# A convolutional feed-forward stage on one NeuronCore: both halves' sample products in one visit, with joins and splits put elsewhere

## The chip, the core and the metric

The kernel runs on one NeuronCore of a Trainium2 chip. A core has five engines that run their own instruction streams: TensorE (PE in the profile; PEld is its weight load), VectorE (DVE), ScalarE (ACT), GpSimd (POOL) and SyncE (SP, which here only issues DMAs). They wait for each other by semaphores. The metric is the device time of one execution in microseconds (us). The kernel before takes 1741.15 us, the median of three runs (1740.54 to 1743.8).

## The reference

One step of a one-layer hybrid decoder: 256 prompt tokens and 64 sample tokens (8 sequences of 8), model width 2048. The first part mixes tokens (a chunked gated MLP beside a state-space scan); the change does not touch its arithmetic. The second part is the convolutional feed-forward, with 5632 hidden columns:

```python
def conv_ffn(h, conv_state, w_up, conv_w, conv_b, w_down):
    up = h @ w_up
    up, new_conv = causal_depthwise_conv(up, conv_state, conv_w, conv_b)
    g, u = jnp.split(up, 2, axis=-1)
    return (jax.nn.gelu(g, approximate=True) * u) @ w_down, new_conv
...
    f, new_ffn_conv = conv_ffn(rms_norm(x, p["norm_ffn_pre"]), ffn_conv_state,
                               p["ffn_w_up"], p["ffn_conv_w"], p["ffn_conv_b"], p["ffn_w_down"])
    x = x + rms_norm(f, p["norm_ffn_post"])
```

Everything is float32. The convolution has three taps; its last two rows of each sequence are outputs too.

## The kernel before

**Products in parts.** A float32 matmul is done as three matmuls of rounded parts. ScalarE rounds a weight slab to its high part (`whi`, line 124), VectorE subtracts to get the low part (`wlo`, line 125), and TensorE adds up high by high, low by high and high by low (lines 135 to 137). `slab` loads a slab on SP's queue; `rounded` and `split_after` put the splits in an order on their engine, with no semaphore.

**Groups.** The feed-forward goes in 11 groups (`NG`) of 4 x 128 hidden columns. `ffn_up(g)` makes the up projection of both halves (gate and value) of group g: 16 parts of 24 matmuls (`ps`). Each finished block of 128 columns goes through `evac`: VectorE scales it out of PSUM into `pad` (lines 1346, 1347), ScalarE and VectorE do the convolution (1353, 1355), GpSimd copies the kept rows (`stg` 1357, `ptf` 1358), and in the value half VectorE multiplies gate and value into the left operand `a` (1363, prompt) and `a_s` (1364, samples). A store of `stg` (1405) stands on ScalarE's queue. `Parts` cuts `a` into four blocks a11, a12, a21, a22 and four sums s1 to s4, each split into a high part on ScalarE (398) and a low part on VectorE (399).

**The down projection** of group g-1 runs between the parts of group g: after each part, `advance` takes one step of the generator `down_steps(g - 1, ...)`. The output has 2048 columns in two halves m. For each half, prompt tokens take seven products instead of eight (a Strassen-like scheme): p1 (a11 by b11), p2 (a12 by b21), p5 (s1 by t1), p7 (s3 by t3), p3 (s4 by b22), p6 (s2 by t2), p4 (a22 by t4). b11 to b22 are blocks of the down weights (128 x 1024 each, on SP's queue); t1 to t4 are differences of them, each made by four subtractions on GpSimd (`less`, line 1512), which are ordered behind the last copy of kept rows (`kept_rows`). One product is `ready` (split of the weights, 1490 and 1491), six matmuls into `pm` (1475), and an add on VectorE into one of seven running sums (`taken_in`, 1469). The sample tokens take no such scheme: at p2's step of each half the raw weights are multiplied by `a_s` in eight matmuls (`pms`, 1482, two records each in the profile). In this text that is a **visit**. Two visits a group, ten groups, make 20.

t3 overwrites b12, t2 overwrites b11 and t4 overwrites b21; b11, b12, b21 and b22 are read by the visit too, so GpSimd makes t2, t3 and t4 only after it.

**The end.** After the last group, `together` joins the seven running sums of each half (seven adds of 128 x 512 on VectorE, line 1567): half 0 after its last product, half 1 at the end of the last `down_steps`. The last group has no later group to hide behind: `down_plain` does its down products straight (lines 1572 and on), with slabs split by line 124 and 125, and the final RMSNorm follows (1700, 1720).

**What sets the order.** Each engine's order is fixed when the program is built, by priorities: `first()` and `tc.high_priority` raise one, `tc.issue_after(x)` puts an instruction behind x on its engine. The lines that the prediction turns on:

```python
for i, (xi, wi) in enumerate(((0, 0), (1, 0), (0, 1))):   # whi by a_hi, whi by a_lo, wlo by a_hi
...
elif j == 3:
    self.cut("a12")
    self.cut("a22")
```

## Time and profile before

The profiled execution took 1738.82 us; its span is 1737.1 us.

| | |
|---|---|
| median, lowest, highest of three runs | 1741.15, 1740.54, 1743.8 us |
| profiled execution, span | 1738.82, 1737.1 us |
| TensorE, VectorE, ScalarE, GpSimd busy | 1722.9, 1363.9, 878.5, 684.8 us |
| sample matmuls `pms`, 320 records | 73.1 us |
| weight subtractions on GpSimd, line 1512, 320 | 351.1 us in three groups |
| DMA traffic | 310.6 MB, 179 GB/s mean |

Rows of a timeline are: start, duration, engine, line, operation, tiles written <- tiles read, shape, count, and in brackets the idle time just before and what ended it. Rows of the chain of waits are: start, time on the chain, engine, tile, line. Rows of the windows are: stretch, its length, then busy time and instructions of PE, PEld, DVE, ACT and POOL, TensorE's granted clock, the DMA share and GB/s. Of two overlapping matmuls each has its own full duration, so the distance of their starts is what one costs.

### The profile page before, as it was taken

What the parts mean: (1) busy time and instruction counts of PE and PEld (TensorE: products, weight loads), DVE (VectorE), ACT (ScalarE), POOL (GpSimd) and SP (SyncE); (2) the same over time, 40 slices, a digit from 0 to 9 for tenths busy, and PEclk for the clock granted to TensorE, in tenths of its full rate; (3) what the DMA queues carried; (4) which work ended last, traced back from release to release, by engine and by line L of the source; (5) the groups of instructions that cost most, each with busy time, mean ns of one, the idle gap of its engine ahead of it and who ended that gap; (6) DMA issues with size and microseconds to landing.
All of it is one profiled execution on the core that took longest, in us unless ns stands there. A gap on an engine that the chain in (4) does not pass through costs nothing.

```text
span 1737.1 us, 29944 instructions
## 1 busy us (share of the span) xinstructions
PE 1722.9 (99%) x11223; PEld 1605.9 (92%) x11223; DVE 1363.9 (79%) x2137; ACT 878.5 (51%) x1272; POOL 684.8 (39%) x999
## 2 busy tenths in 40 slices
PE   9999999999999999999999999999999999999997
PEld 9999999999999999999988898888888889888884
DVE  6549864657969788788987778888887879798898
ACT  6344545333656565645565444444444444454443
POOL 2432230000423423112355556565655555555552
PEclk9999999999999999999999999999999999999999
DMA  8786664556676777665765544545445454545445
GB/s 265 215 240 184 185 177 148 157 163 191 202 225 197 227 221 220 205 199 164 241 185 156 158 147 148 159 142 178 150 145 171 144 166 150 164 149 160 148 143 161
DMA packets 216018, 310.60 MB, mean 179 GB/s; under 512 B 22080, under 2 KB 118976, under 8 KB 215680
## 3 DMA queue, kind: packets, MB, share of 16 engines
q1 hardware_dynamic: 198624, 279.76, 53.1%
q0 software_dynamic: 6176, 13.87, 2.6%
q10 hardware_dynamic: 11072, 15.05, 2.5%
q8 instruction: 88, 1.44, 0.4%
q14 instruction: 58, 0.48, 0.1%
HBM read 285.00 MB, written 22.32 MB: 177 GB/s over the span
## 4 chain that ended last, share of the span: by engine, by line
PE 96%; DVE 2%; issue 1%; ACT 0%; POOL 0%; DVEq 0%; ACTq 0%; POOLq 0%
PE ps L135 20%; PE ps L137 20%; PE ps L136 20%; PE pm L1475 11%; PE pd L135 4%; PE pd L137 4%; PE pd L136 4%; PE pms L1482 4%; PE y_ps L1088 1%; PE ps_v L135 1%; PE ps_v L136 1%; PE ps_v L137 1%; DVE wlo L125 0%; PE yo_ps L1003 0%; PE up_ps L1020 0%
## 5 line engine op out<-in xcount | busy, mean ns | idle before, releaser
L135 PE MATMUL ps<-h_hi,whi 128*128 128x320 f32 x2428 | 750.2, 309 | 0.0
L137 PE MATMUL ps<-h_hi,wlo 128*128 128x320 f32 x2428 | 749.0, 309 | 0.1
L136 PE MATMUL ps<-h_lo,whi 128*128 128x320 f32 x2428 | 748.6, 308 | 0.0
L125 DVE TENSOR_TENSOR wlo<-wraw,whi 128x1024 fp32r<-128x1024 f32 (+2 forms) x394 | 487.4, 1238 | 146.0 <-ACT whi L124 144.2
L124 ACT CAST whi<-wraw 128x1024 fp32r<-128x1024 f32 (+2 forms) x393 | 405.1, 1031 | 372.9 <-PE ps L136 143.1
L135 PEld LDWEIGHTS ps<-h_hi,whi 128*128 128x128 f32 x2428 | 455.6, 188 | 9.1 <-issue 1.3
L136 PEld LDWEIGHTS ps<-h_lo,whi 128*128 128x128 f32 x2428 | 455.9, 188 | 6.3
L137 PEld LDWEIGHTS ps<-h_hi,wlo 128*128 128x128 f32 x2428 | 455.5, 188 | 0.7 <-DVE wlo L125 0.6
L1491 DVE TENSOR_TENSOR wlo<-b,whi 128x1024 fp32r<-128x1024 f32 x120 | 155.1, 1292 | 74.4 <-ACT whi L1490 74.2
L1490 ACT CAST whi<-b 128x1024 fp32r<-128x1024 f32 x120 | 125.5, 1046 | 161.9 <-PE ps L136 144.1
L1512 POOL TENSOR_TENSOR b<-b,b 128x256 f32<-128x256 f32 x160 | 184.8, 1179 | 0.0
L135 PE MATMUL pd<-ohi,whi 128*128 128x320 f32 x448 | 138.7, 310 | 0.0
L137 PE MATMUL pd<-ohi,wlo 128*128 128x320 f32 x448 | 138.3, 309 | 0.0
L136 PE MATMUL pd<-olo,whi 128*128 128x320 f32 x448 | 138.3, 309 | 0.0
L1358 POOL COPY ptf<-pad 128x2 f32<-128x2 f32 x88 | 39.2, 446 | 187.2 <-DVE pad L1346 186.6
L1512 POOL TENSOR_TENSOR b<-b,t 128x256 f32<-128x256 f32 x80 | 76.8, 969 | 86.0 <-PE pms L1482 86.0
L1512 POOL TENSOR_TENSOR t<-b,b 128x256 f32<-128x256 f32 x80 | 89.5, 1148 | 14.7 <-DMA b<-in_ffn_w_down 14.7
L135 PEld LDWEIGHTS pd<-ohi,whi 128*128 128x128 f32 x448 | 84.1, 188 | 0.6
L136 PEld LDWEIGHTS pd<-olo,whi 128*128 128x128 f32 x448 | 84.1, 188 | 0.3
L137 PEld LDWEIGHTS pd<-ohi,wlo 128*128 128x128 f32 x448 | 84.1, 188 | 0.0
L248 DVE TENSOR_TENSOR acc_mix<-acc_mix,pd 128x320 f32<-128x320 f32 (+1 forms) x113 | 53.7, 478 | 27.8 <-PE pd L137 27.5
L1482 PE MATMUL pms<-b,a_s 128*64 128x512 f32 x320 | 73.1, 598 | 0.0
(415 smaller groups left out, 2490.4 us busy)
## 6 DMA issues: line engine op xcount, KB each, us to landing
wraw<-in_ffn_w_up SPq DMA_DIRECT2D x176, 512.0 KB, 4.5
wraw<-in_w_in SPq DMA_DIRECT2D x132, 512.0 KB, 3.9
b<-in_ffn_w_down SPq DMA_DIRECT2D x80, 512.0 KB, 4.5
wraw<-in_w_out SPq DMA_DIRECT2D x64, 512.0 KB, 3.5
st<-in_state_ssm SPq DMA_DIRECT2D x40, 256.0 KB, 4.4
out_ssm_state_sample<-st ACTq DMA_DIRECT2D x30, 256.0 KB, 2.4
cs<-dacs_d SPq DMA_DIRECT2D x16, 320.0 KB, 5.3
wraw<-in_w_in SPq DMA_DIRECT2D x12, 384.0 KB, 4.3
```

The source lines that it names most:

```text
L124: rounded[:] = [act.copy(hi, raw).ins]
L125: lowered[:] = [dve.tensor_tensor(out=lo, in0=raw, in1=hi.bitcast(F32), op=ALU.subtract).ins]
L135: pe.matmul(ps, whi, xhi, start=first, stop=False)
L136: pe.matmul(ps, whi, xlo, start=False, stop=False)
L137: last_made[0] = pe.matmul(ps, wlo, xhi, start=False, stop=last).ins
L248: added_last[:] = [dve.tensor_tensor(out=acc[:, nb, ts], in0=acc[:, nb, ts], in1=ps[:, ts], op=ALU.add).ins]
L1358: kept_rows[:] = [pool.tensor_copy(ptf[:, k, :], pad[:, 256:258]).ins]
L1475: last_made[0] = pe.matmul(ps, x[xi][:, k], w[wi][:, 512 * k:512 * k + 512], start=start and k + i == 0, stop=stop and k == 1 and i == 2).ins
L1482: last_made[0] = pe.matmul(ps[64 * h:64 * h + 64], a_s[:, k0 + k], w[h][:, 512 * k:512 * k + 512], start=start and k == 0, stop=stop and k ...
L1490: rounded[:] = [act.copy(hi, raw).ins]
L1491: dve.tensor_tensor(out=lo, in0=raw, in1=hi.bitcast(F32), op=ALU.subtract)
L1512: pool.tensor_tensor(out=to[:, cs], in0=raw[x][:, cs], in1=raw[y][:, cs], op=ALU.subtract)
```

## The change

1. **One visit a group.** Both halves' sample products are done at the second half's p2 step, 16 matmuls. So the first half's four weight blocks stay unwritten until then: t1 to t4 go to tiles of their own (`one`, `two`), and the second half's b11 lies in an extension of the first running sums' tile (`beside`), b12 and b22 in the two `gain` tiles, b21 in t1's tile. Their loads are issued at the end of the first half's steps.
2. **Weight differences behind the last copy of kept rows.** The `ptf` copy now comes ahead of the `stg` copy, and `less` is ordered behind the latter.
3. **Joins one or two to a step.** The joins of the last `down_steps` are put into its steps, each with `first()`; the last group's evacuations of blocks 2 and 3 of the value half are ordered behind the latest one.
4. **Last chunk.** Slab splits from the fourth on are ordered behind the last left operand's split; the last group's two stores of kept rows wait for its first split on ScalarE; the loads of the norm's gain move into the last `down_steps`; raw tiles are used in another order.
5. Four scratch tiles of the earlier part (`sq`, `s`, `zs`) come from another pool, which frees room in SBUF.

The diff, without the moves of item 5:

```diff
@@ -1332,7 +1333,11 @@
             parts = Parts(a, a_s, g == NG - 1)
 
             def evac(half, j, ps):
-                with first() if g == NG - 1 and half == 1 else nullcontext():
+                with ExitStack() as how:
+                    if g == NG - 1 and half == 1:
+                        how.enter_context(first())
+                        if j >= 2:
+                            how.enter_context(tc.issue_after(taken[0]))
                     convolved(half, j, ps)
 
             def convolved(half, j, ps):
@@ -1354,8 +1359,8 @@
                 for r in range(1, 3):
                     dve.scalar_tensor_tensor(out=t[:, :n], in0=pad[:, r:r + n], scalar=col(prm_at[f"fw{r}"][0] + k), in1=t[:, :n],
                                              op0=ALU.mult, op1=ALU.add)
-                pool.tensor_copy(stg[:, half, j], tokp[:, :, 8:10])
-                kept_rows[:] = [pool.tensor_copy(ptf[:, k, :], pad[:, 256:258]).ins]
+                with tc.issue_after(pool.tensor_copy(ptf[:, k, :], pad[:, 256:258]).ins):
+                    kept_rows[:] = [pool.tensor_copy(stg[:, half, j], tokp[:, :, 8:10]).ins]
                 if half == 0:
                     gelu[:] = [act.activation(t[:, :n], t[:, :n], AF.Gelu_apprx_tanh).ins]
                     return
...
@@ -1402,7 +1407,8 @@
 
             for half in range(2):
                 k = NF * half + 4 * g
-                act.dma_start(o_fconv_s[:, k:k + 4], stg[:, half])
+                with tc.issue_after(parts.made[0]) if g == NG - 1 else nullcontext():
+                    act.dma_start(o_fconv_s[:, k:k + 4], stg[:, half])
             return parts
 
         eps = fp.tile([P, 1], F32, name="eps")
@@ -1453,11 +1460,13 @@
 
         nxt = ffn_up(0)
 
-        sums_of_m, f_s, taken = [None, None], [None, None], []
+        sums_of_m, f_s, taken, beside, gain = [None, None], [None, None], [], [], []
 
         def room_for_sums(m):
 
-            room = fp.tile([P, 8, 512], F32, name="in_fp") if m else hp.tile([P, 8, 512], F32, tag="acc_mix", name="in_mix")
+            room = fp.tile([P, 8, 512], F32, name="in_fp") if m else hp.tile([P, 10, 512], F32, tag="acc_mix", name="in_mix")
+            if m == 0:
+                beside.append(room[:, 8:10].rearrange("p i n -> p (i n)"))
             sums_of_m[m] = [room[:, i] for i in range(7)]
             f_s[m] = room[:, 7]
 
@@ -1492,88 +1501,119 @@
...
+            def samples():
+                ps = [misc("pms") for _ in range(2)]
+                for h in range(2):
+                    raw = raws[h]
+                    sample_products(ps[h], parts.a_s, 0, (raw["b11"], raw["b12"]), True, False)
+                    sample_products(ps[h], parts.a_s, 2, (raw["b21"], raw["b22"]), False, True)
+                for h in range(2):
+                    taken_in(f_s[halves[h]], ps[h], ck == 0)
+
...
-                for name in ("b11", "b12", "b22", "b21"):
-                    load(name)
-                product(1, "a11", "b11")
+            for name in ("b11", "b12", "b22", "b21"):
+                load(0, name, fp.tile([P, 1024], F32, name=name))
+            for h in range(2):
+                raw = raws[h]
+                last = h and ck == NG - 2
+                if last:
+                    together(0, 0)
+                product(h, 1, "a11", "b11")
                 yield
-                raw["t1"] = fp.tile([P, 1024], F32, name="t1")
-                less(raw["t1"], "b12", "b11")
-                ps = misc("pms")
-                sample_products(ps, parts.a_s, 0, (raw["b11"], raw["b12"]), True, False)
-                sample_products(ps, parts.a_s, 2, (raw["b21"], raw["b22"]), False, True)
-                taken_in(f_s[m], ps, ck == 0)
-                product(2, "a12", "b21")
+                one = fp.tile([P, 1024], F32, tag="t2" if h else "t1", name="one")
+                less(h, "t1", "b12", "b11", one)
+                if h:
+                    samples()
+                if last:
+                    together(0, 1)
+                product(h, 2, "a12", "b21")
                 yield
-                raw["t3"] = raw["b12"]
-                less(raw["t3"], "b22", "b12")
-                product(5, "s1", "t1")
+                two = beside[0] if h else fp.tile([P, 1024], F32, tag="t2", name="two")
+                less(h, "t3", "b22", "b12", two)
+                if last:
+                    together(0, 2)
+                product(h, 5, "s1", "t1")
                 yield
-                raw["t2"] = raw["b11"]
-                less(raw["t2"], "b22", "t1")
-                product(7, "s3", "t3")
-                if ck == 0 and m == 1:
+                less(h, "t2", "b22", "t1", one)
+                if last:
+                    together(0, 3)
+                product(h, 7, "s3", "t3")
+                if ck == 0 and h == 0:
                     with tc.issue_after(lowered[0]):
                         to_rows(2)
                 yield
-                raw["t4"] = raw["b21"]
-                less(raw["t4"], "t2", "b21")
-                product(3, "s4", "b22")
-                if ck == 0 and m == 1:
+                less(h, "t4", "t2", "b21", two)
+                if last:
+                    together(0, 4, 5)
+                product(h, 3, "s4", "b22")
+                if ck == 0 and h == 0:
                     with tc.issue_after(lowered[0]):
                         to_rows(3)
+                if last:
+                    with tc.issue_after(slab_load[-1]):
+                        for m in range(2):
+                            gain.append(fp.tile([P, SN, 4, 32], F32, tag="gain", name="gain", bufs=2).rearrange("p s k f -> p (s k f)"))
+                            sp.dma_start(gain[m][:, :1024], norm_last[0:1, 1024 * m:1024 * m + 1024].broadcast_to([P, 1024]))
                 yield
-                product(6, "s2", "t2")
+                if last:
+                    together(0, 6)
+                    together(1, 1)
+                product(h, 6, "s2", "t2")
+                if h == 0:
+                    if ck == 0:
+                        room_for_sums(halves[1])
+                    load(1, "b11", beside[0])
+                    for name in ("b12", "b22"):
+                        load(1, name, fp.tile([P, SN, 4, 32], F32, tag="gain", name=name, bufs=2).rearrange("p s k f -> p (s k f)")[:, :1024])
                 yield
-                product(4, "a22", "t4")
-                if ck == NG - 2 and m == 0:
-                    together(0)
+                if last:
+                    together(1, 0, 2, 3, 4)
+                product(h, 4, "a22", "t4")
+                if h == 0:
+                    load(1, "b21", fp.tile([P, 1024], F32, tag="t1", name="b21"))
+                if last:
+                    together(1, 5, 6)
                 yield
-            if ck == NG - 2:
-                together(1)
-                yield
 
...
-        def together(m):
+        def together(m, *which):
             t = [None] + sums_of_m[m]
...
+            sums = ((6, 1, ALU.add), (2, 1, ALU.add), (7, 6, ALU.add), (6, 5, ALU.add), (3, 6, ALU.add), (4, 7, ALU.subtract), (7, 5, ALU.add))
+            for n in which:
+                x, y, op = sums[n]
+                with first(), tc.issue_after(taken[0]):
+                    taken[:] = [dve.tensor_tensor(out=t[x], in0=t[y], in1=t[x], op=op).ins]
+            if 6 in which:
+                for c, n, i in ((0, 0, 2), (0, 1, 3), (1, 0, 4), (1, 1, 7)):
+                    f[c][2 * m + n] = t[i]
@@ -1597,7 +1637,8 @@
                             kept = [fp.tile([P, 1024], F32R, tag=t, name="kept") for t in ("b11", "b12")]
                         elif (nb, i) in ((1, 1), (3, 1)):
                             kept = [held_w[:, nb - 1], held_w[:, nb]]
-                        raw = None if 3 <= n < 6 else fp.tile([P, 1024], F32, tag=("t1", "b22", "b21")[n % 6], name="raw")
+                        raw = None if 3 <= n < 6 else fp.tile([P, 1024], F32, tag=("b22", "b21", "t1")[n % 6], name="raw")
+                        split_after.append(parts.made if n >= 3 else None)
                         slab(rows_of(ffn_w_down, 4 * ck + 2 * i, 2, 512 * nb, 512), kept=kept, room=raw)
                         w = tuple(kept or both[1:])
                         raws.append(both[0])
@@ -1658,11 +1698,6 @@
             nxt = ffn_up(g)
             while bg:
                 advance(bg, steps)
-            if g == 4:
-                with tc.issue_after(slab_load[-1]):
-                    for m in range(2):
-                        gain.append(fp.tile([P, SN, 4, 32], F32, tag="gain", name="gain", bufs=2).rearrange("p s k f -> p (s k f)"))
-                        sp.dma_start(gain[m][:, :1024], norm_last[0:1, 1024 * m:1024 * m + 1024].broadcast_to([P, 1024]))
 
         held_w = hp.tile([P, 4, 1024], F32R, tag="h_hi", name="held_w")
         gain_s = hp.tile([P, 1024], F32, tag="ohi", name="gain_s")
@@ -1756,7 +1791,8 @@
         with tc.issue_after(gelu[0]):
             act.activation(fp.tile([P, 1], F32, name="root_ready"), eps, AF.Sqrt)
         down_plain(NG - 1, nxt, one_block, load_x1)
-        act.dma_start(o_fconv_p, ptf)
+        with tc.issue_after(nxt.made[0]):
+            act.dma_start(o_fconv_p, ptf)
 
 
 _OUTS = [
```

The orders of three engines at the start of the group whose weights are b_12648 (b11), b_12650 (b12), b_12652 (b22) and b_12654 (b21). In the trace this is the group with its first product at 1203.19 us, and the other six from 1036.55 to 1536.47 us stand alike.

TensorE, before, between two parts at p2's step of the first half:

```order
L137 MATMUL ps_3_12557<-h_hi,wlo 128x320
L1482 MATMUL pms<-b_12648,a_s 64x512
L1482 MATMUL pms<-b_12650,a_s 64x512
L1482 MATMUL pms<-b_12648,a_s 64x512
L1482 MATMUL pms<-b_12650,a_s 64x512
L1482 MATMUL pms<-b_12654,a_s 64x512
L1482 MATMUL pms<-b_12652,a_s 64x512
L1482 MATMUL pms<-b_12654,a_s 64x512
L1482 MATMUL pms<-b_12652,a_s 64x512
L1475 MATMUL pm<-whi,a_hi 128x512
L1475 MATMUL pm<-whi,a_lo 128x512
```

In the changed kernel p2 stands directly behind the part:

```order
L137 MATMUL ps_3_12557<-h_hi,wlo 128x320
L1484 MATMUL pm<-whi,a_hi 128x512
L1484 MATMUL pm<-whi,a_lo 128x512
L1484 MATMUL pm<-wlo,a_hi 128x512
L1484 MATMUL pm<-whi,a_hi 128x512
```

The eight matmuls between are now in the second half's visit, ahead of eight of its own.

GpSimd, before, from the last copies of kept rows on (`t_12698` is t1; `b_12650<-b_12652,b_12650` is t3):

```order
L1358 COPY ptf<-pad 128x2
L1512 TENSOR_TENSOR t_12698<-b_12650,b_12648 128x256 x4
L1357 COPY stg<-pad 128x16
L1343 MEMSET pad 128x2
L1344 COPY pad<-fst 128x8x2
L1343 MEMSET pad 128x2
L1344 COPY pad<-fst 128x8x2
L1343 MEMSET pad 128x2
L1344 COPY pad<-fst 128x8x2
L1512 TENSOR_TENSOR b_12648<-b_12652,t_12698 128x256
L1512 TENSOR_TENSOR b_12650<-b_12652,b_12650 128x256 x2
```

And in the changed kernel (first `one` is t1, first `two` is t3):

```order
L1362 COPY ptf<-pad 128x2
L1363 COPY stg<-pad 128x16
L1519 TENSOR_TENSOR one<-b_12650,b_12648 128x256 x4
L1519 TENSOR_TENSOR two<-b_12652,b_12650 128x256 x4
L1348 MEMSET pad 128x2
L1349 COPY pad<-fst 128x8x2
L1348 MEMSET pad 128x2
L1349 COPY pad<-fst 128x8x2
L1348 MEMSET pad 128x2
L1349 COPY pad<-fst 128x8x2
L1519 TENSOR_TENSOR one<-b_12652,one 128x256 x4
```

The stg copy moved ahead of t1, and t3's four subtractions moved up behind t1's.

VectorE, in the changed kernel, up to the split of a12 (the first of `a_lo ... x2`):

```order
L1443 TENSOR_TENSOR s<-a 128x256
L1443 TENSOR_TENSOR s<-s,a 128x256
L1500 TENSOR_TENSOR wlo<-b_12654,whi 128x1024
L1478 TENSOR_TENSOR in_mix<-in_mix,pm 128x512
L125 TENSOR_TENSOR wlo<-wraw,whi 128x1024
L399 TENSOR_TENSOR a_lo<-a,a_hi 128x256 x2
L1443 TENSOR_TENSOR s<-a,s 128x256
L399 TENSOR_TENSOR s_lo<-s,s_hi 128x256 x2
L1500 TENSOR_TENSOR wlo<-one,whi 128x1024
L1478 TENSOR_TENSOR in_mix<-in_mix,pm 128x512
```

These rows stand as before (with other line numbers); only the add of `pms`, which followed behind them, is gone from here.

More of the change, by code (lines that the diff above doesn't have):

```diff
@@ L105, in first @@
         return tc.high_priority(offset=200000)
-    slab_load, split_after, both, rounded, lowered = [], [None], [], [], []
+    slab_load, split_after, both, rounded, lowered, copied = [], [None], [], [], [], []
     def slab(src, half=0, begins=False, kept=None, room=None):
@@ L328, in add_square @@
         else:
-            sq = tp.tile([P, NT], F32, tag=place[0], name="sq", bufs=place[1])
+            sq = mixer[0].tile([P, NT], F32, tag=place[0], name="sq", bufs=place[1])
             act.activation(sq, x, AF.Square)
@@ L347, in step @@
                 else:
-                    one.append(tp.tile([P, NT], F32, tag="sq", name="sq", bufs=2))
+                    one.append(mixer[0].tile([P, NT], F32, tag="sq", name="sq", bufs=2))
                 for ts in parts_of(nb):
@@ L397, in split @@
         if scale is None:
-            act.copy(hi, x)
+            copied[:] = [act.copy(hi, x).ins]
             made = dve.tensor_tensor(out=lo, in0=x, in1=hi.bitcast(F32), op=ALU.subtract)
@@ L1494, in down_steps, with load @@
             last_rows = kept_rows[0]
+            halves = (1, 0) if ck == 0 else (0, 1)
+            raws = [{}, {}]
+            def load(h, name, room):
+                k, n = int(name[1]) - 1, int(name[2]) - 1
+                raws[h][name] = room
+                with tc.high_priority(offset=100000), tc.issue_after(slab_load[-1]) if ck == 0 else nullcontext():
+                    sp.dma_start(room.rearrange("p (k n) -> p k n", n=512),
+                                 rows_of(ffn_w_down, 4 * ck + 2 * k, 2, 1024 * halves[h] + 512 * n, 512))
@@ new lines, in less, with product @@
+            def less(h, to, x, y, room):
+                raw = raws[h]
+                with tc.high_priority(offset=100000), tc.issue_after(last_rows):
+                    for q in range(0, 1024, 256):
+                        cs = slice(q, q + 256)
+                        pool.tensor_tensor(out=room[:, cs], in0=raw[x][:, cs], in1=raw[y][:, cs], op=ALU.subtract)
+                raw[to] = room
+            def product(h, i, x, w):
+                hi, lo = ready(raws[h][w])
+                ps = misc("pm")
+                prompt_products(ps, (parts.hi[x], parts.lo[x]), (hi, lo), True, True)
+                taken_in(sums_of_m[halves[h]][i - 1], ps, ck == 0)
@@ L1558, in down_steps @@
+                yield
+                if last:
[5 more added lines that the diff above has]
+                    together(1, 5, 6)
                 yield
         f = [[None] * 4 for _ in range(2)]
-        def together(m):
+        def together(m, *which):
             t = [None] + sums_of_m[m]
-            def plus(x, y, op=ALU.add):
-                with tc.issue_after(taken[0]):
-                    dve.tensor_tensor(out=t[x], in0=t[y], in1=t[x], op=op)
-            plus(6, 1)
-            plus(2, 1)
-            plus(7, 6)
-            plus(6, 5)
-            plus(3, 6)
-            plus(4, 7, ALU.subtract)
-            plus(7, 5)
-            for c, n, i in ((0, 0, 2), (0, 1, 3), (1, 0, 4), (1, 1, 7)):
-                f[c][2 * m + n] = t[i]
+            sums = ((6, 1, ALU.add), (2, 1, ALU.add), (7, 6, ALU.add), (6, 5, ALU.add), (3, 6, ALU.add), (4, 7, ALU.subtract), (7, 5, ALU.add))
[6 more added lines that the diff above has]
+                    f[c][2 * m + n] = t[i]
```

33 lines of the change are left out of this document (9 added, 24 removed).

## The prediction

> **What bounds the kernel now.** I read the page first, then the windows by stage, the chain of waits, and the timelines of TensorE, VectorE and GpSimd at the places the change touches.
>
> ```profile
> PE 1722.9 (99%) x11223; PEld 1605.9 (92%) x11223; DVE 1363.9 (79%) x2137; ACT 878.5 (51%) x1272; POOL 684.8 (39%) x999
> PE 96%; DVE 2%; issue 1%; ACT 0%; POOL 0%; DVEq 0%; ACTq 0%; POOLq 0%
> 873.00:1600.00 727.00, 727.00 (x4352) 645.32 (x4352) 602.92 (x841) 357.42 (x447) 412.50 (x568) 1.00 0.51 157
> ```
>
> TensorE (PE) is the bound, and in the stage that the change edits (873 to 1600 us, the feed-forward groups) it is busy for all 727.00 us. So a matmul less there is time gained one to one, and a wait put before a matmul there is time lost one to one, with nothing behind it to win it back. VectorE is second, 602.92 of 727.00 us, so it has little room wherever its work comes in a lump.
>
> **The visits.** Per half, the sample products are 16 records in one piece between two parts of other work. The chain at the start of the group whose first product is at 1203.19:
>
> ```profile
> 1203.19 1.39 PE pm L1475 x6
> 1208.09 3.58 PE pms L1482 x16
> 1211.67 1.60 PE pm L1475 x6
> 1216.79 1.39 PE pm L1475 x6
> ```
>
> A visit costs 3.58, and the product after it 1.60 instead of 1.39, so 3.79 us. Inside, two records go together:
>
> ```profile
> 1208.50 0.60 PE L1482 MATMUL pms<-b,a_s 128*64 128x512 f32 x2
> 1208.93 0.60 PE L1482 MATMUL pms<-b,a_s 128*64 128x512 f32 x2
> 1209.36 1.89 PE L1482 MATMUL pms<-b,a_s 128*64 128x512 f32 x8
> ```
>
> 0.43 us per pair, eight pairs 3.44, so entering and leaving cost 3.79 - 3.44 = 0.35 us. The change does 32 records in one visit: 0.35 us less in each of nine groups. In the order of the new program the first group's visit is still in two pieces (13 matmuls, then 3 after other work), so it saves nothing. **Visits: 9 x 0.35 = -3.15 us.** That is all TensorE saves; its matmuls are the same in number.
>
> **What the first visit was covering.** The second product of a half (a12 by b21, "p2") came behind the visit. Now it comes directly behind the part before it. The step from product to product without a visit is 1216.79 - 1211.67 - 0.21 = 4.91 us, so p2 starts at 1203.19 + 4.91 = 1208.10, where before it came at 1211.67. Its second matmul multiplies whi by the low half of a12, 0.23 us later: it needs a_lo at 1208.33. VectorE (DVE) makes that a_lo here:
>
> ```profile
> 1207.95 1.22 DVE L125 TENSOR_TENSOR wlo<-wraw,whi 128x1024 fp32r<-128x1024 f32 x1
> 1209.09 0.42 DVE L399 TENSOR_TENSOR a_lo<-a,a_hi 128x256 fp32r<-128x256 f32 x1
> 1036.55 1.39 PE pm L1475 x6
> 1042.44 1.28 DVE L399 TENSOR_TENSOR a_lo<-a,a_hi 128x256 fp32r<-128x256 f32 x2
> 1536.47 1.39 PE pm L1475 x6
> 1542.37 1.29 DVE L399 TENSOR_TENSOR a_lo<-a,a_hi 128x256 fp32r<-128x256 f32 x2
> ```
>
> It ends at 1209.51: 1.18 us after p2 now wants it, where the visit used to hide that (ready 2.4 us before the old need). The third and fourth rows and the last two show the same distance, 5.9 us from first product to a_lo, in the first and the last of the seven groups from 1036.55 to 1536.47 in steps of 83.3 us. VectorE's order there is unchanged by the change: the low weights of p2, an add, the low weights of a slab, then a_lo. What is late next is the slab part behind p2, whose low weights come before a_lo and so add nothing.
>
> Can VectorE be there earlier? Only by losing a wait ahead of it:
>
> ```profile
> 1199.00:1209.50 10.50, 10.50 (x67) 9.19 (x67) 10.40 (x22) 7.29 (x12) 3.03 (x5) 1.00 0.24 75
> 1198.56 0.57 DVE L1355 SCALAR_TENSOR_TENSOR ucv<-pad,prm,ucv 128x336 f32<-128x336 f32 x1 [0.57 <-ACT ucv L1353]
> 1197.86 0.67 ACT L1353 ACTIVATE ucv<-pad,prm 128x336 f32<-128x336 f32 x1 [4.37 <-POOL stg L1357]
> ```
>
> It is busy 10.40 of 10.50 us to that point. One wait, 0.57, is for ScalarE (ACT), which stood behind a store that waited for GpSimd's stg copy. The change puts that copy ahead of the weight subtractions, so the 0.57 and the 0.1 of small gaps go: -0.67.
>
> But the change also frees the third weight difference of the half (t3) from waiting for the visit, and gives it a tile of its own. Its four GpSimd (POOL) subtractions now run straight behind t1's four, where before they came at 1209:
>
> ```profile
> 1192.17 4.84 POOL L1512 TENSOR_TENSOR t<-b,b 128x256 f32<-128x256 f32 x4
> 1209.18 0.92 POOL L1512 TENSOR_TENSOR b<-b,t 128x256 f32<-128x256 f32 x1 [3.75 <-PE pms L1482]
> 1190.13 1.22 DVE L125 TENSOR_TENSOR wlo<-wraw,whi 128x1024 fp32r<-128x1024 f32 x1
> 1192.25 1.74 DVE L125 TENSOR_TENSOR wlo<-wraw,whi 128x1024 fp32r<-128x1024 f32 x1
> 1193.91 0.67 DVE L1469 TENSOR_TENSOR in_fp<-in_fp,pm 128x512 f32<-128x512 f32 x1
> 1194.51 1.21 DVE L125 TENSOR_TENSOR wlo<-wraw,whi 128x1024 fp32r<-128x1024 f32 x1
> 1195.65 0.75 DVE L1364 TENSOR_TENSOR a_s<-ucv,gcv 128x64 f32<-128x64 f32 x1
> 1200.64 0.22 DVE L1364 TENSOR_TENSOR a_s<-ucv,gcv 128x64 f32<-128x64 f32 x1
> ```
>
> While GpSimd subtracts, a VectorE operation on two SBUF tiles loses about 0.53: wlo takes 1.74 instead of 1.22, a_s 0.75 instead of 0.22; the add out of PSUM stays at 0.67. Four more subtractions between 1197 and 1202, where VectorE has only operations of the first kind and no gap, delay everything behind by up to 4 x 0.53 = 2.1.
>
> [...]
>
> So a_lo is late by 1.18, less 0.67, plus 0 to 2.1, and a matmul after a wait costs 0.11 more (0.50 against 0.39 in the tail's rows below). The stall is 0.6 us a group if nothing contends, 1.3 if VectorE's clock does not move at all, 2.7 if all four subtractions hit. I take three of the four, nearer the upper end because VectorE has no gap there: 1.18 - 0.67 + 1.6 + 0.11 = 2.2, rounded up to 2.3 for the hand-over of 0.04. **Seven groups: 7 x 2.3 = +16.1 us** (bounds +4 and +19).
>
> The first, the second and the tenth group have their split earlier, and pay nothing:
>
> ```profile
> 873.28 1.39 PE pm L1475 x6
> 877.37 0.75 DVE L399 TENSOR_TENSOR a_lo<-a,a_hi 128x256 fp32r<-128x256 f32 x2
> 953.21 1.40 PE pm L1475 x6
> 953.58 0.75 DVE L399 TENSOR_TENSOR a_lo<-a,a_hi 128x256 fp32r<-128x256 f32 x2
> 1616.27 1.39 PE pm L1475 x6
> 1617.83 0.76 DVE L399 TENSOR_TENSOR a_lo<-a,a_hi 128x256 fp32r<-128x256 f32 x2
> ```
>
> a_lo starts 4.1, 0.4 and 1.6 us after the first product there, not 5.9, and ends before p2's second matmul 5.14 after it.
>
> **The loads.** The second half's weights get rooms of their own. The last to come free is b21's (t1's tile, once the product before the last has split it), two steps of 4.9 us before its own split is due, against
>
> ```profile
> b<-in_ffn_w_down SPq DMA_DIRECT2D x80, 512.0 KB, 4.5
> ```
>
> 4.5 us to land: hidden. Not in the first group: there b22 of the second half stands on SP's queue behind two loads of the next group, whose rooms the visit itself frees (its third and fourth matmul, 1.8 us in). Three loads then land together, 4.5 to 7.5 us later by the same row and its spread, 6.3 to 9.3 us into the visit; its last three matmuls want b22 after 13 x 0.45 + 1.4 + 1.3 = 8.6 us. **+0.5 us** (0 to 3).
>
> **The joins, the splits and the queues of the tail.** The joins (14 adds of 128x512 on VectorE) move from the last group's end into the steps before; the last chunk's slab splits stand behind its left operand; two stores on ScalarE's queue wait for the first split.
>
> ```profile
> 1679.57 0.50 PE L1475 MATMUL pm<-wlo,s_hi 128*128 128x512 f32 x1 [1.12 <-DVE wlo L1491]
> 1701.79 0.50 PE L1475 MATMUL pd<-whi,a_lo 128*128 128x512 f32 x1 [0.67 <-DVE a_lo L399]
> 1702.13 0.39 PE L1475 MATMUL pd<-wlo,a_hi 128*128 128x512 f32 x1
> 1725.67 0.40 PE L1475 MATMUL pd<-held_w,a_hi 128*128 128x512 f32 x1
> 1727.38 0.68 DVE L1700 TENSOR_TENSOR in_fp<-in_fp,pd 128x512 f32<-128x512 f32 x1
> ```
>
> To be had: the wait for a_lo at the last chunk (0.67 and 0.11), the 1.12 and its 0.11, and the last add, which starts 1.3 us behind TensorE's last matmul (1725.67 + 0.40), because VectorE still clears joins: 3.3 us in all, 4 with what is smaller. To be lost: joins of 0.68 now stand ahead of the low weights of the last group's last slab parts, and each one ahead of a wlo that is due makes TensorE wait 0.6. Three to five of them do, 2 to 3 us, in place of the 1.12. **Net -1.5 us** (-4 to +1.5).
>
> The rest costs nothing: the ring of tiles that moved pools holds the same work, and the stores wait on ScalarE's queue, busy 51%, behind splits that come first anyway.
>
> **Sum:** -3.15 + 16.1 + 0.5 - 1.5 = +12 on the profiled execution: its 1738.82 us (span 1737.1 and 1.7 around it) become 1750.8. That execution lies 2.3 below the median shown, 1741.15, so the median becomes **1753 us**.
>
> **Rivals.** (1) *The subtractions do not contend*, because VectorE's operations slip between them as the wlo at 1194.51 did with 1.21 us. For it: that one of the two wlo beside t1's four subtractions lost nothing. Against: the operations beside t3's are shorter and more, so more of them meet a subtraction. The stalls are then 0.6 to 1.3: 7 x 0.6 = 4.2 to 9.1, totals of 0 to +5, 1741 to 1746, say 1743.5. (2) *Faster: VectorE is ahead by the time p2 comes.* ScalarE waited 4.37 us behind the stg copy; if its earlier start pulls the evacuation forward by more than the 1.18 needed at 1209.51, no p2 waits, and what is left is -3.15 + 0.5 - 1.5 = -4.1, 1737. Against it: VectorE itself waited only 0.57 for that, and was busy 10.40 of 10.50 afterwards. It decides from 1.2 us of lead on. (3) *Worse at both ends*: all four contend (7 x 2.8 = 19.6), b22 3 us late, and the tail a loss of 1.5: +21, 1762. (4) *The change does not do what it says*: the scheduler still splits the visit, as in the first group; the order shows it whole in nine, so that is only the 0.35 already left out.
>
> **How the numbers follow.** The forecast 0.50 (its own range 1747 to 1759), rival 1 0.26, rival 2 0.17, rival 3 0.07. A median of this kernel can be told from no change at about 0.2%, 3.5 us. Slower: the forecast but for 0.03, half of rival 1, rival 3: 0.67. Same: half of rival 1, 0.03 of the forecast, 0.02 of rival 2: 0.18. Faster: 0.15. The range goes down to rival 2's 1737 and up to 1760, near rival 3.
>
> **What would show it.** In the new profile: the chain has one piece of 32 sample records a group; TensorE's list of waits, which had three entries of about 1 us, shows pm waiting for a_lo some seven times, 1 to 3 us each, 83 us apart, each about 4.9 us behind a group's first product; t3's subtractions run directly behind t1's, and wlo, a_lo or ucv operations of VectorE beside them take 0.5 more. TensorE's busy time falls by about 3 us while the span grows. I am wrong if no wait for a_lo shows there, or if it shows and the time still falls.

## The result, and the profile after

The changed kernel takes 1766.09 us (median of 4, 1764.27 to 1766.2), the kernel before 1740.85: a ratio of 1.014, 95% interval 1.0122 to 1.0157. It is slower by 25 us, where 12 were forecast; 1766 lies outside the range of 1737 to 1760. The profiled execution took 1766.15 us, its span 1764.4.

The page, then TensorE's list of waits (engine, tile, line, what it waited for: us in total, times, longest), then the stage 873 to 1600 us of the windows:

```profile
PE 1729.2 (98%) x11223; PEld 1608.7 (91%) x11223; DVE 1363.6 (77%) x2137; ACT 876.5 (50%) x1272; POOL 644.9 (37%) x999
```

```profile
PE ps L137 <- DVE wlo L125: 11.3, 12, 3.6
PE pm L1484 <- DVE a_lo L399: 10.3, 7, 1.5
...
PE pms L1491 <- DMA b<-in_ffn_w_down: 0.9, 1, 0.9
PE spread L298 <- DVE rs_r L282: 0.8, 1, 0.8
```

```profile
873.00:1600.00 727.00, 708.61 (x4232) 629.97 (x4233) 587.98 (x822) 348.25 (x439) 359.83 (x548) 1.00 0.50 152
```

TensorE, busy for all 727.00 us of that stage before, now stands still for 18.4 of them. The matmuls are the same 11223, but busy time rose by 6.3 us: a matmul before a gap shows its full 0.31 us, where otherwise the next, 0.147 later, covers half of it, and some matmuls near the end run at a granted clock of 0.50 (last section).

Where the 27.3 us of span came from is read off the first product of a group. TensorE's timeline, before and after, first `pm` matmul of groups 1, 2, 3 and 10, and of the tenth's second half:

```profile
873.12 0.39 PE L1475 MATMUL pm<-whi,a_hi 128*128 128x512 f32 x1
953.05 0.40 PE L1475 MATMUL pm<-whi,a_hi 128*128 128x512 f32 x1
1036.38 0.39 PE L1475 MATMUL pm<-whi,a_hi 128*128 128x512 f32 x1
1616.10 0.39 PE L1475 MATMUL pm<-whi,a_hi 128*128 128x512 f32 x1
1654.24 0.39 PE L1475 MATMUL pm<-whi,a_hi 128*128 128x512 f32 x1
```

```profile
874.88 0.39 PE L1484 MATMUL pm<-whi,a_hi 128*128 128x512 f32 x1
958.86 0.40 PE L1484 MATMUL pm<-whi,a_hi 128*128 128x512 f32 x1
1043.52 0.39 PE L1484 MATMUL pm<-whi,a_hi 128*128 128x512 f32 x1
1639.76 0.39 PE L1484 MATMUL pm<-whi,a_hi 128*128 128x512 f32 x1
1675.43 0.39 PE L1484 MATMUL pm<-whi,a_hi 128*128 128x512 f32 x1
```

| stretch | before | after | more | forecast, visits included |
|---|---|---|---|---|
| up to the first group's first product | 873.12 | 874.88 | +1.8 | 0 |
| first group | 79.93 | 83.98 | +4.1 | +0.5 |
| second group | 83.33 | 84.66 | +1.3 | -0.35 |
| third to ninth, seven steady groups | 579.72 | 596.24 | +16.5 | +13.7 |
| tenth group to the end of the span | 121.0 | 124.64 | +3.6 | -1.85 |

In a steady group (first product at 1214.87; before, at 1203.03) TensorE waits twice. The rows show the first product before, then TensorE after, then VectorE and GpSimd in the same stretch:

```profile
1203.03 0.39 PE L1475 MATMUL pm<-whi,a_hi 128*128 128x512 f32 x1
```

```profile
1214.87 0.39 PE L1484 MATMUL pm<-whi,a_hi 128*128 128x512 f32 x1
...
1217.40 0.41 PE L137 MATMUL ps<-h_hi,wlo 128*128 128x320 f32 x1 [0.70 <-DVE wlo L125]
...
1220.73 0.40 PE L1484 MATMUL pm<-whi,a_hi 128*128 128x512 f32 x1
1222.61 0.50 PE L1484 MATMUL pm<-whi,a_lo 128*128 128x512 f32 x1 [1.48 <-DVE a_lo L399]
```

```profile
1207.66 2.99 DVE L1360 SCALAR_TENSOR_TENSOR ucv<-pad,prm,ucv 128x336 f32<-128x336 f32 x3
1210.56 0.95 DVE L1368 TENSOR_TENSOR a<-ucv,gcv 128x256 f32<-128x256 f32 x1
1211.44 1.76 DVE L1500 TENSOR_TENSOR wlo<-b,whi 128x1024 fp32r<-128x1024 f32 x1
1213.12 0.75 DVE L1369 TENSOR_TENSOR a_s<-ucv,gcv 128x64 f32<-128x64 f32 x1
...
1222.13 0.75 DVE L399 TENSOR_TENSOR a_lo<-a,a_hi 128x256 fp32r<-128x256 f32 x2
```

```profile
1204.15 5.16 POOL L1519 TENSOR_TENSOR one<-b,b 128x256 f32<-128x256 f32 x4
1209.28 4.51 POOL L1519 TENSOR_TENSOR two<-b,b 128x256 f32<-128x256 f32 x4
```

Beside t3's four subtractions (`two`, from 1209.28) four VectorE operations are each about 0.53 longer: wlo 1.76 instead of 1.23, a_s 0.75 instead of 0.22, a 0.95 instead of 0.42, and the three ucv together 2.99 instead of the 2.50 of e1 below. Beside t1's four, just before, not every operation pays: the wlo at 1204.10 and at 1205.84, with an add out of PSUM between them, keep their 1.23 and 1.22. a_lo starts 7.26 us after the first product, where before it was 6.06 (1209.09 less 1203.03). Counted by the starts of the matmuls and with the slower restart behind each (0.1: the rows have 0.41 and 0.50, where the same matmuls without a wait have 0.31 and 0.39), the first wait costs 0.96 us and the second 1.74, together 2.7; less 0.35 for the visit that is 2.35, and 16.5 / 7 = 2.36 a group were measured. (The expectations below have 1.64 for the second, without its restart.)

### The profile page after: what moved, and what is told of

Same layout as the page of the kernel before. It is cut to its first block, busy times and chain, and to the rows that moved or that the text cites. A ratio compares the mean times of both kernels' runs of the same rounds, so it can differ in the third digit from the quotient of the medians.

```text
span 1764.4 us, 29885 instructions
## 1 busy us (share of the span) xinstructions
PE 1729.2 (98%) x11223; PEld 1608.7 (91%) x11223; DVE 1363.6 (77%) x2137; ACT 876.5 (50%) x1272; POOL 644.9 (37%) x999
## 4 chain that ended last, share of the span: by engine, by line
PE 82%; DVE 12%; issue 2%; DMA 2%; ACT 1%; SPq 0%; DVEq 0%; ACTq 0%
PE ps L135 17%; PE ps L137 16%; PE ps L136 16%; PE pm L1484 9%; PE pd L135 4%; PE pd L136 4%; PE pd L137 4%; PE pms L1491 4%; DVE wlo L125 3%; DVE ucv L1360 2%; DVE wlo L1500 2%; DVE a L1368 1%; DMA wraw<-in_ffn_w_up 1%; DVE a_s L1369 1%; PE pd L1484 1%
## 5 line engine op out<-in xcount | busy, mean ns | idle before, releaser
L137 PE MATMUL ps<-h_hi,wlo 128*128 128x320 f32 x2428 | 751.9, 310 | 11.4 <-DVE wlo L125 11.3
L135 PEld LDWEIGHTS ps<-h_hi,whi 128*128 128x128 f32 x2428 | 456.4, 188 | 10.3 <-issue 2.1
L1519 POOL TENSOR_TENSOR one<-b,one 128x256 f32<-128x256 f32 x80 | 71.3, 923 | 109.3 <-DVE wlo L1500 107.0
L1362 POOL COPY ptf<-pad 128x2 f32<-128x2 f32 x88 | 43.7, 497 | 171.3 <-DVE pad L1351 170.5
L1500 DVE TENSOR_TENSOR wlo<-b,whi 128x1024 fp32r<-128x1024 f32 x50 | 71.5, 1430 | 29.9 <-ACT whi L1499 29.9
L1499 ACT CAST whi<-b 128x1024 fp32r<-128x1024 f32 x50 | 52.3, 1046 | 63.6 <-PE ps L136 59.3
L1500 DVE TENSOR_TENSOR wlo<-one,whi 128x1024 fp32r<-128x1024 f32 x40 | 48.9, 1222 | 32.8 <-ACT whi L1499 32.8
L1015 POOL TENSOR_TENSOR st<-st,tote 128x512 f32<-128x512 f32 x32 | 45.5, 1450 | 61.3 <-DMA st<-in_state_ssm 38.4
```

The costliest lines, as they stand in the source:

```text
L135: pe.matmul(ps, whi, xhi, start=first, stop=False)
L137: last_made[0] = pe.matmul(ps, wlo, xhi, start=False, stop=last).ins
L1015: pool.tensor_tensor(out=by_head(st[h]), in0=by_head(st[h]), in1=tote[:, h0:h0 + 8, 4 * h + i:4 * h + i + 1].to_broadcast([P, 8, 64]), op= ...
L1499: rounded[:] = [act.copy(hi, raw).ins]
L1500: dve.tensor_tensor(out=lo, in0=raw, in1=hi.bitcast(F32), op=ALU.subtract)
L1519: pool.tensor_tensor(out=room[:, cs], in0=raw[x][:, cs], in1=raw[y][:, cs], op=ALU.subtract)
```

## The experiments

Theory A: the missing visit uncovers a_lo, and t3's subtractions, now beside VectorE's lump of work, make it later. Rival B: only the missing cover counts. For the first group and the end each has an experiment of its own. Each ran beside the kernel before, which took 1741.5 us beside e1 to e4, 1740.7 beside e5 to e8, 1740.14 beside e9 and e10, and 1740.85 beside the changed kernel. "Less than the changed kernel" compares medians that were not taken side by side, and those of the kernel before differ by 1.4 us, so a difference of that size says little alone; where it matters, the stretches of the profiles are given too.

**e1: t3's subtractions later.** In `less`, for the first half's t3:

```diff
-                with tc.high_priority(offset=100000), tc.issue_after(last_rows):
+                behind = last_rows
+                if (h, to) == (0, "t3"):
+                    with tc.high_priority(offset=100000), tc.issue_after(last_rows):
+                        behind = pool.tensor_copy(marker, parts.lo["a22"][:, 0, 0:1].bitcast(F32)).ins
+                with tc.high_priority(offset=100000), tc.issue_after(behind):
```

> The changed kernel, with the first half's t3 subtractions held on GpSimd until the split of a22's low half is there (a one-column copy of that low half stands ahead of them), so that they no longer run beside VectorE's work just before a12's split. [...] Rival B (only the lost cover counts, contention is small): the a_lo wait stays at 1.3 or more and the time at 1762 or above.

By theory A the two waits of a steady group fall from 2.6 us to 0.5, 7 x 2.1, and 3 us go in the other three groups: 17.7 less, about 1748. Measured: 1746.9 us, 19.2 less than the changed kernel (ratio to before 1.0032, 1.0019 to 1.0045). The waits, and VectorE in the group whose a_lo the wait is for (its first product at 1207.70):

```profile
PE ps L137 <- DVE wlo L125: 4.0, 3, 3.6
PE pm L1484 <- DVE a_lo L399: 2.1, 7, 0.3
```

```profile
1203.25 1.21 DVE L1500 TENSOR_TENSOR wlo<-b,whi 128x1024 fp32r<-128x1024 f32 x1
1204.39 0.21 DVE L1369 TENSOR_TENSOR a_s<-ucv,gcv 128x64 f32<-128x64 f32 x1
...
1212.84 0.75 DVE L399 TENSOR_TENSOR a_lo<-a,a_hi 128x256 fp32r<-128x256 f32 x2
```

wlo and a_s have their short times back, and a_lo starts 5.14 us after the first product. So the contention is worth 7.26 - 5.14 = 2.12 us, four times 0.53. What is left against the kernel before, 6.06 - 5.14 = 0.92, I put down to the earlier stg copy; no run takes that copy alone. Rival B falls.

**e2: two visits again,** with t3 still early:

```diff
-                if h:
-                    samples()
+                samples(h)
```

(`samples` then takes one half.)

> The changed kernel with the sample products of each half back in that half (two visits a group), all else kept, t3's early subtractions too. Theory A: the visit covers a_lo again, so 7 x 1.64 = 11.5 us go, the waits of about 1 us for a slab's low weights behind the first product stay in all ten groups, the visits cost 3.2 us more, the first group's wait for b22 (about 1 us) goes: about 1757. Rival B: the waits behind the first product go too, because they belong to the missing visit: about 1748.

Measured: 1758.77 us, 1.8 more than expected; the first and the second group take 5.4 and 2.0 us more than before.

```profile
PE ps L137 <- DVE wlo L125: 12.2, 12, 3.8
```

No wait for a_lo is left in the list; that behind the first product stays, with the visit in its old place. So it is the contention's alone, and the wait for a_lo is the missing visit's and the contention's together.

**e3: a12's split first.** In `Parts.there`:

```diff
-                    self.cut("a12")
+                    with first():
+                        self.cut("a12")
```

> The changed kernel with the split of a12 raised in priority, which puts its low half on VectorE ahead of an add and the low weights of a slab (0.68 + 1.22 us earlier). Theory A: the wait of 1.64 us for a_lo goes, the slab part behind the second product waits some 0.3 us instead, the 0.96 us behind the first product stays: 7 x 1.35 = 9.4 us less, about 1757. Rival B (the place in VectorE's order does not matter, the wait only moves to the slab part behind): no change, 1764 to 1767.

Measured: 1754.44 us, 11.7 less than the changed kernel, of which the profiles show 10.2 in the seven steady groups (596.2 to 586.1 us) and 1.0 at the end, where this profile, unlike the others with the wait of 3.55 us, shows no fall of the clock (1.00; last section); no wait for a_lo in the list, and 11.3 us in 12 waits for slabs' low weights as before the edit. The rival falls: the place in VectorE's order matters, and the cost it moves to the slab behind is small.

**e4: the end as before.**

```diff
-                    together(0, 0)
...
+                if ck == NG - 2 and h == 0:
+                    together(0, *range(7))
...
-                        if j >= 2:
-                            how.enter_context(tc.issue_after(taken[0]))
...
-                        split_after.append(parts.made if n >= 3 else None)
```

> The changed kernel with the end as before: joins in two lots, the last chunk's splits and the two stores not ordered behind its left operand, raw tiles in the old order. The trace of the changed kernel shows 2.7 us lost from the last group's second half to the end, by a wait of 3.55 us for a slab's low weights behind joins and 1.4 us of slow matmuls after it, against 1.9 us gained: if that is the joins' doing, about 1763.4. By the prediction's step (the new end gains 1.5): about 1767.6.

Measured: 1763.96 us, 2.1 less than the changed kernel. From the first product of the tenth group's second half to the end of the span the profiles show 89.0 us in the changed kernel, 87.3 in e4, and 82.8 before, where the first half's visit of 3.44 is not yet in it (86.3 with it). The end of the change is a loss, not a gain. In the changed kernel VectorE and TensorE stand like this there:

```profile
1703.50 1.28 DVE L1613 TENSOR_TENSOR in_mix<-in_mix 128x512 f32<-128x512 f32 x2
1704.71 0.74 DVE L399 TENSOR_TENSOR a_lo<-a,a_hi 128x256 fp32r<-128x256 f32 x2
1705.38 0.67 DVE L1478 TENSOR_TENSOR in_fp<-in_fp,pm 128x512 f32<-128x512 f32 x1
1705.97 0.68 DVE L1613 TENSOR_TENSOR in_mix<-in_mix 128x512 f32<-128x512 f32 x1
1706.58 0.68 DVE L1613 TENSOR_TENSOR in_fp<-in_fp 128x512 f32<-128x512 f32 x1
1707.18 1.21 DVE L125 TENSOR_TENSOR wlo<-wraw,whi 128x1024 fp32r<-128x1024 f32 x1
```

```profile
1708.44 0.41 PE L137 MATMUL ps<-h_hi,wlo 128*128 128x320 f32 x1 [3.55 <-DVE wlo L125]
```

Four joins (L1613), the split of a block that is not due yet and an add stand ahead of the low weights that TensorE waits for from 1704.9 on.

**e5: e1 and e3 together.**

> The two edits of e1 and e3 together: t3's subtractions held until a22's low half is there, and a12's split ahead in VectorE's order. Theory A: what was left of the waits in e1 (0.3 us for a_lo with 0.11 behind it and 0.1 of small ones, in seven groups) goes, so a steady group costs TensorE 0.35 us less than before: 7 x 0.55 = 3.9 us below e1's 1746.9, about 1743. What stays above the kernel before is the first group (2 us) and the end (2 to 3 us). Rival (the edits help by the same place, so they do not add): 1746 to 1747.

Measured: 1744.88 us (1.0024, 1.0015 to 1.0033), 2.0 below e1 where 3.9 were expected. In its list of waits nothing is left for a_lo. By their first products in the profiles, the seven steady groups take 577.8 us, where e1's take 581.2 and those of the kernel before 579.7: 3.4 less than e1, so the edits do add, and 1.9 less than before, where 7 x 0.35 = 2.45 were to be had. The middle is mended; what costs still is the two ends.

**e6: e5 with the end as before, and the first group with two visits** and the old rooms:

```diff
+                if ck == 0:
+                    samples(h)
+                elif h:
+                    samples(0, 1)
...
+                    if ck == 0:
+                        for name in ("b11", "b12", "b22"):
+                            load(1, name, fp.tile([P, 1024], F32, name=name))
```

> e5 with the end as before (e4's edit), and the first group with two visits and the kernel before's rooms for its second half's weights, so that their loads wait for neither the norm's gain tiles nor the next group's loads. Theory A, with the first group's loss of about 2 us put down to b22's late load: 1743 - 2.1 (e4's measured share of the end) - 2.2 + 0 = about 1738.7, a little below the kernel before by nine groups' 0.35 us. If the first group's loss has another cause: about 1741.

Measured: 1739.21 us (0.9994, 0.9986 to 1.0003): no difference from before that can be told.

**e7: e6 with the change's splits behind the left operand kept.** Against e6:

```diff
+                        split_after.append(parts.made if n >= 3 else None)
...
+                with tc.issue_after(parts.made[0]) if g == NG - 1 else nullcontext():
```

> e6 with the change's order of the last chunk's splits and stores kept (behind the last left operand). The changed kernel's trace shows 0.7 us gained at the last chunk's first products: 0.5 to 0.8 us below e6, about 1738. If the splits ordered behind the left operand come too late for the slabs after: 0.5 to 1 us above e6.

Measured: 1737.85 us (0.9986, 0.9977 to 0.9995), 1.4 below e6, in medians of 11 runs each. The waits of TensorE of 1.2 us for a product's low weights and of 0.2 for a_lo in e6's profile are gone. e7 also keeps the change's order of the raw tiles, so this part of the change, the three orders together, is a gain at the end.

**e8: e7 with the joins spread, at ordinary priority.** Against the changed kernel's end:

```diff
-                with first(), tc.issue_after(taken[0]):
-                    taken[:] = [dve.tensor_tensor(out=t[x], in0=t[y], in1=t[x], op=op).ins]
+                with tc.issue_after(taken[0]):
+                    dve.tensor_tensor(out=t[x], in0=t[y], in1=t[x], op=op)
...
-                        if j >= 2:
-                            how.enter_context(tc.issue_after(taken[0]))
```

> e7 with the joins spread over the steps as in the change, but at ordinary priority and without ordering the last evacuations behind them, so that no join stands ahead of a slab's low weights that is due. If the loss at the end came from the joins' priority and not from spreading them: no wait of 3.55 us, and the last add no longer 1.3 us behind TensorE: about 1 us below e7, 1737. If spreading itself is the loss: 1740 or above.

Measured: 1736.84 us, ratio 0.9974, interval 0.9965 to 0.9984: 0.26% faster than the kernel before. Its whole list of waits of TensorE:

```profile
PE early L69 <- DVE ones L65: 1.1, 1, 1.1
PE ps L137 <- DVE wlo L125: 0.8, 3, 0.4
PE spread L298 <- DVE rs_r L282: 0.2, 1, 0.2
```

**e9: the changed kernel with the first group alone mended** (e6's second edit).

> The changed kernel with the first group alone mended: two visits there, and its second half's weights loaded into the kernel before's rooms. The changed kernel loses 4.1 us between the first products of the first and the second group; 1.3 of it is a slab part's wait behind t1's and t3's subtractions, which stays. If the rest belongs to the late b22 and the visit in two pieces, 2.7 us go: about 1763.4. If only the 0.88 us wait for the load counts: about 1765.

Measured: 1762.4 us, 3.7 less. From first product to first product the first group takes 1.5 us more than before instead of 4.1, so 2.5 of the 3.7 are seen there. The changed kernel has this there, the piece of the visit that stands alone:

```profile
926.49 1.93 PE L1491 MATMUL pms<-b,a_s 128*64 128x512 f32 x6 [0.88 <-DMA b<-in_ffn_w_down]
```

The edit took the wait for the load and the split visit away together; it does not part the one from the other.

**e10: the changed kernel with its joins at ordinary priority** (the two edits shown at e8; the joins are then no longer ordered behind one another either).

> The changed kernel with its joins at ordinary priority, and the last evacuations not ordered behind them; all else kept. If the joins' priority is what makes TensorE wait 3.55 us for a slab's low weights and run slowly after it, both go, with the gains of the end kept: 27.4 - 24.6 = 2.7 us of loss become a gain of about 1.5 as in e8: about 4.2 us less, 1762. If the low weights are late for another reason (slab splits or GpSimd): 1765 or above.

Measured: 1759.9 us, 6.2 less, more than the 4.2 expected. The profiles show 4.5 of it from the tenth group's second half to the end (89.0 to 84.5 us); 1.1 more lies up to the end of the first group, which the edit does not touch. The longest wait for low weights is 1.0 us now:

```profile
PE ps L137 <- DVE wlo L125: 8.1, 12, 1.0
```

## Why the prediction was right in kind, wrong in size, and wrong in sign at the end

**Where the forecast was short.** The span grew by 27.3 us, some 15 more than the +12. By the table, 5.5 of that lie from the tenth group to the end, 3.6 in the first group, 2.8 in the steady groups, 1.7 in the second group and 1.8 ahead of the first.

**What bounds the kernel, and the visits.** Right, and 3 us is all that could be won in the middle. In e5 and e6 the seven steady groups are 0.27 us shorter than before on average, in e7 and e8 0.17 and 0.13. Single groups are either 0.36 shorter, as worked out, or as long as before. In the latter one and the same slab matmul starts 0.2 to 0.27 us late and the one behind it 0.1, too little for the list of waits. In e8 its step is 0.37 instead of 0.147:

```profile
1156.17 0.30 PE L136 MATMUL ps<-h_lo,whi 128*128 128x320 f32 x1
1156.54 0.41 PE L137 MATMUL ps<-h_hi,wlo 128*128 128x320 f32 x1
```

**What the first visit was covering.** Right in mechanism, a little small: 2.3 us a group were forecast (bounds 0.6 and 2.7), 2.7 measured. I took three of four subtractions as hitting; all four do, 2.12 us. VectorE is 0.92 earlier without them, not 0.67. But the reading of "what is late next" failed. It named the wrong slab part: the low weights that came late first are those of the part right behind the first product, 0.96 us, which VectorE makes before a12's split. That the sum came out near all the same is owed to the second wait: TensorE's first wait shortens the wait for a_lo behind it, so the two together are still a_lo's lateness.

**The second and tenth group "pay nothing".** Wrong. Their a_lo is early, but their slab part behind the first product waits 0.9 and 0.7 us (1.2 and 1.0 by the starts of the matmuls), as the first group's does with 0.95: t3's subtractions are early in all of them. I looked for the wait only where the visit was gone. That is most of the 1.3 us of the second group, and one of the tenth; in e1, 0.8 to 1.0 us of it is gone in both.

**The loads of the first group: +0.5.** Too small. The load's own wait is 0.9, inside the bounds (0 to 3), but the group's excess is 4.1: about 2.5 went with the rooms and the split visit (e9), and the 1.5 left are mostly the slab part's wait, which the forecast did not have.

**The tail: -1.5.** This is the step that failed in sign. I forecast 3.3 to 4 us of gains against 2 to 3 of losses, each of three to five joins ahead of due low weights at 0.6. The joins do stand there, but four of them stand ahead of one and the same wlo, together with a split and an add, so TensorE waits 3.55 in one piece; and it ran slowly afterwards, 1.5 more (last section), which the sum did not have. The loss is then 5.0 and more, and the stretch to the end is 2.7 longer than before (89.0 against 86.3), where it should have been 1.5 shorter. The gains I named are there, if smaller: without the priority, spread joins and late splits are worth 2.4 us against the old end (e6 to e8). So the part that failed is the joins' priority with the orders that hang on it, 4.5 us at the end (e10). No run parts the priority from those orders; what speaks for it is where the joins stand in VectorE's rows under e4.

**The rivals.** The result lies nearest rival 3, every bound at its bad end at once (1762, chance 0.07), and 4 us beyond it. I treated the bounds of steady groups, loads and end as if they would average out, but nothing makes them do so. They have causes of their own, each with an experiment (e1, e9, e10). Two of the three are of one kind: work put ahead on VectorE (the joins, with a wait of 3.55 us behind them), or beside it (t3's subtractions, 2.12 us a group), was paid where VectorE's results were due.

**What stays open.** The 1.8 us up to the first group's first product. Part of it is the wait of 0.8 for rs_r; profiles of the ten experiments show between -0.1 and 1.8 there with the same pools, and none of the edits was made for it. The second group stays 0.34 us longer than before in e5 to e8, with a wait of 0.25 for a slab's low weights left in it. And e9 leaves the load and the split visit together.

**The checks named beforehand.** The seven waits for a_lo are there, 10.3 us in total, in the product 5.9 us behind a group's first instead of 4.9, and t3's subtractions run directly behind t1's. TensorE's busy time did not fall by 3 us: it rose by 6.3, with gaps of 18.4 us in the stage, so here it is no measure of saved work.

## What to carry to other kernels

Before a block of matmuls is moved away, list what becomes ready behind it: the block was 3.6 us of cover, and it hid 1.2 us of lateness that no list of waits shows. Work taken off another engine's wait (here t3's subtractions, which no longer waited for the visit) did not vanish but ran earlier, beside something else; ask which engine's operations it lengthens at that time (here VectorE's, four of them by 0.53 us each), and price it at every place where that engine's results are due, not only at the place of the edit. Ask too what stands behind work whose priority is raised: the joins, which nobody waited for, stood ahead of low weights that TensorE waited 3.55 us for.

## What the runs showed of the hardware

In the changed kernel TensorE's granted clock fell from 1.00 to 0.50 after the wait of 3.55 us, some 1.4 us after it had resumed, for 3.4 us. The windows (stretch, length, busy time of PE, PEld, DVE, ACT, POOL, granted clock, DMA share, GB/s), of the changed kernel and then of e3 and of e6:

```profile
1708.40:1710.00 1.60, 1.56 (x10) 1.56 (x11) 1.60 (x2) 0.00 (x0) 0.00 (x0) 0.94 0.35 36
1710.00:1712.90 2.90, 2.90 (x13) 2.90 (x12) 0.66 (x1) 0.00 (x0) 0.00 (x0) 0.50 0.68 210
```

```profile
1698.00:1700.90 2.90, 2.90 (x20) 2.73 (x19) 0.95 (x2) 1.21 (x2) 0.00 (x0) 1.00 0.79 238
```

```profile
1722.00:1725.40 3.40, 3.40 (x10) 2.65 (x9) 3.26 (x10) 0.73 (x3) 0.00 (x0) 0.50 0.58 216
```

Matmuls that start 0.147 us apart elsewhere start 0.267 apart in the second stretch: eleven such steps, and with the two at the edges 1.5 us lost beside the wait itself.

The length of the wait alone does not settle it. e1, e2, e3, e5 and e9 keep a wait of 3.55 to 3.8 us at that place. In e5 the clock is at 0.50 from the moment TensorE resumes, in e2 from 0.8 us later, each for 3.4 us; in e1 and e9 from more than 1 us before it resumes, for 6.8 us; and in e3 it stays at 1.00 (second fence, from 1.5 us after the wait's end at 1696.47). In e6 it is at 0.50 for 3.4 us, from 0.7 us behind the end of a wait of only 1.72 (third fence), while the changed kernel's seven waits for a_lo, the longest 1.48, have no such trail (1.00 from 873 to 1600 us). So this cost differs between profiles by a us or two for a reason that no edit set.
